# Attention stages of a two-layer trunk: accumulation banks by segment, a bank of their own for the value sums, and two places for other work per step

## The chip, the cores and the metric

The kernel runs on one core of one Trainium2 chip. The metric is the device time of one execution in microseconds (us); the time before is the median of three runs. TensorE is called PE, VectorE DVE, ScalarE ACT, GpSimd POOL, SyncE SP.

## What is computed

Two layers over 256 context tokens and 512 latent tokens, 1024 channels, all in 32-bit floats. Cut to what matters here:

```python
for l in range(2):
    h = rmsnorm(x) * (1 + scale) + shift               # latent and context tokens
    u, q, k, v, hq, hi, zf, zb, hgate, g_pool, g_attn, g_hg = split(h @ w_in[l])
    q, k = rope(rmsnorm(q)), rope(rmsnorm(k))            # 8 query heads of 64, 2 key heads
    a = softmax(q k^T / 8) v                             # latent queries: all 768 keys; context queries: 256
    y = (sigmoid(g_pool) * (pool_mix(u) @ w_bp) + sigmoid(g_attn) * (a @ w_ba)
         + sigmoid(g_hg) * (hgrn(hq, hi, zf, zb, hgate) @ w_bh)) @ w_out[l]
    x = x + gate * y
    x = x + gate2 * swiglu(rmsnorm(x) * (1 + scale2) + shift2)
```

In layer 0 both token groups are carried on (T = 768 columns); of layer 1 only the latent tokens are wanted (512 columns).

## The kernel before

Activations are kept transposed, 128 channels by tokens, so a product is a sum over eight tiles of 128 channels. Each 32-bit factor is split into a rounded part `hi` and a rest `lo` (ACT casts, DVE subtracts, `load_w` and `split`), and a product takes three matmuls (`mm3`, L261): hi x hi, lo x hi, hi x lo. One output tile of 128 channels over 512 columns is therefore 24 matmuls, and `gemm_h` gives control back after each three.

PE's order is written out by hand: PE executes in the order of the program. The other engines are ordered by a scheduler. To keep PE busy while DVE and ACT work, the program keeps a queue of other products: the branch products of the recurrent mixer (`merge` with `w_bh`, tiles `boh`) and the gate products of the attention branch (`early_gates`), whose tanh is stored to DRAM (`tdr`) and read back in the last merge. `fill(us)` issues as many from the queue as the cost says; the amounts are in the table `PACE`.

There are eight PSUM banks of 512 columns. The pool `pa` (tag "att") has four; the pool `pg` (tag "g") holds two double banks for a product over both segments in layer 0 (`wide`), and four single banks in layer 1.

Attention goes over four pairs of heads p. For a pair, `attn_pv` walks over jobs, one for each block of 128 keys and, in layer 0, one for the context queries: `score` (four matmuls, L673 and L674, then the exponential on ACT, L675), `hooks`, then `value` (the sums with v, L683, into one bank of `pa` that is held for the whole pair). Within `hooks(i)`, once per step, stands what belongs to the next pair: the split of its queries (`attn_max` to its first yield, L607 on ACT), its score maxima over the context keys (L620, four matmuls of 256 columns into two banks, then two reduces L622 on DVE) and over the latent keys (L628, two of 512 columns, reduces L630), two such pieces in each of steps 0 to 3 and the rest in step 4; then the maxima's rows (L646), the next projection of queries, and the filler.

After the last pair, `attn_out` sums the exponentials (L763, copied on ACT L764), divides and splits (L273 and L274) into `boa`. Then the last `merge` (`w_ba`) goes over eight output tiles: tanh of the gate (from DRAM, or from a gate product made there where none was ready), 12 branch matmuls, a product with the gate on DVE (L825), an addition on POOL (L827) to the sum so far that is read back from DRAM (`ybuf`), and a split into `y`. The output projection (`grouped`, L1064) needs all eight y for each of its tiles.

## Time and profile before

| | |
|---|---|
| median of 3 runs | 2167.5 us (2167.08 to 2168.65) |
| the profiled execution's own time | 2168.29 us |
| its span | 2166.5 us |
| PE busy | 2087.3 us (96%) |
| DVE, ACT, POOL busy | 51%, 32%, 7% |
| layer 0's attention steps | some 398 to 579 us |
| layer 1's attention steps | some 1559 to 1712 us |
| layer 1's last merge, then the output projection | from 1720 us, from 1753.4 us |

A row of a timeline is one instruction: when it starts, how long its record lasts, and in brackets how long its engine stood idle before it and what ended that. Records of matmuls overlap: what a matmul costs in a stream is the distance between starts. A row of waits is a sum over a stretch.

### The profile page before, as it was taken

What the parts mean: (1) busy time and instruction counts of PE and PEld (TensorE: products, weight loads), DVE (VectorE), ACT (ScalarE), POOL (GpSimd) and SP (SyncE); (2) the same over time, 40 slices, a digit from 0 to 9 for tenths busy, and PEclk for the clock granted to TensorE, in tenths of its full rate; (3) what the DMA queues carried; (4) which work ended last, traced back from release to release, by engine and by line L of the source; (5) the groups of instructions that cost most, each with busy time, mean ns of one, the idle gap of its engine ahead of it and who ended that gap; (6) DMA issues with size and microseconds to landing.
All of it is one profiled execution on the core that took longest, in us unless ns stands there. A gap on an engine that the chain in (4) does not pass through costs nothing.

```text
span 2166.5 us, 28558 instructions
## 1 busy us (share of the span) xinstructions
PE 2087.3 (96%) x11844; PEld 1696.6 (78%) x11844; DVE 1102.7 (51%) x1615; ACT 691.2 (32%) x968; POOL 147.4 (7%) x153
## 2 busy tenths in 40 slices
...
GB/s 280 89 30 103 187 164 90 50 69 59 109 121 143 88 138 161 101 88 156 139 66 106 91 81 74 57 65 97 88 73 63 111 188 86 96 98 93 99 93 97
DMA packets 74018, 226.74 MB, mean 105 GB/s; under 512 B 8272, under 2 KB 8416, under 8 KB 73760
## 3 DMA queue, kind: packets, MB, share of 16 engines
...
## 4 chain that ended last, share of the span: by engine, by line
PE 85%; DVE 7%; ACT 3%; DMA 2%; issue 2%; POOL 1%; SPq 0%; POOLq 0%; DVEq 0%; ACTq 0%
PE g L261 63%; PE g L1064 5%; PE att L683 3%; PE att L367 2%; PE g L1020 2%; PE att L1064 2%; DMA ada<-in_w_ada_dram 2%; PE att L673 1%; PE att L424 1%; DVE AT L463 1%; PE att L674 1%; PE att L173 1%; PE att L628 1%; DVE lo L243 1%; PE att L1020 1%
## 5 line engine op out<-in xcount | busy, mean ns | idle before, releaser
L261 PE MATMUL g<-h,hi 128*128 128x512 f32 (+1 forms) x3840 | 991.9, 361 | 9.1 <-ACT h L319 2.6
L261 PEld LDWEIGHTS g<-h,hi 128*128 128x128 f32 x3840 | 680.1, 189 | 146.9 <-issue 26.0
L261 PE MATMUL g<-h,lo 128*128 128x512 f32 (+1 forms) x1920 | 571.1, 355 | 0.2 <-DVE lo L243 0.2
L241 ACT CAST hi<-raw 128x1024 fp32r<-128x1024 f32 (+1 forms) x237 | 245.3, 1036 | 830.1 <-PE g L261 526.1
L243 DVE TENSOR_TENSOR lo<-raw,hi 128x1024 fp32r<-128x1024 f32 (+1 forms) x237 | 285.4, 1206 | 330.2 <-ACT hi L241 327.6
L261 PEld LDWEIGHTS g<-h,lo 128*128 128x128 f32 x1920 | 363.3, 189 | 53.2 <-issue 1.7
L261 PE MATMUL g<-uh,hi 128*128 128x512 f32 (+1 forms) x416 | 130.4, 360 | 0.0
L261 PE MATMUL g<-ul,hi 128*128 128x512 f32 (+1 forms) x416 | 130.4, 360 | 0.0
L261 PE MATMUL g<-uh,lo 128*128 128x512 f32 (+1 forms) x416 | 130.3, 360 | 0.0
L1078 DVE SCALAR_TENSOR_TENSOR x<-g,mod,x 128x256 f32<-128x256 f32 (+1 forms) x64 | 42.4, 682 | 166.5 <-PE g L261 146.8
L980 DVE TENSOR_TENSOR sa<-sa,g 128x512 f32<-128x512 f32 (+1 forms) x43 | 35.1, 818 | 171.1 <-PE g L261 169.9
L675 ACT ACTIVATE e<-att 128x512 f32<-128x512 f32 x104 | 56.6, 595 | 124.5 <-PE att L674 124.5
L214 DVE SCALAR_TENSOR_TENSOR junk<-adar,cb 128x1024 f32<-128x1024 f32 x64 | 78.2, 1222 | 34.1 <-DMA adar<-in_w_adaT_dram 33.2
L261 PEld LDWEIGHTS g<-ul,hi 128*128 128x128 f32 x416 | 78.2, 188 | 12.5
L261 PEld LDWEIGHTS g<-uh,lo 128*128 128x128 f32 x416 | 78.2, 188 | 12.4
L261 PEld LDWEIGHTS g<-uh,hi 128*128 128x128 f32 x416 | 78.2, 188 | 12.4
L827 POOL TENSOR_TENSOR ybuf<-ybuf,tanh 128x768 f32<-128x768 f32 (+1 forms) x32 | 57.8, 1807 | 388.9 <-DVE tanh L825 261.2
L324 POOL TENSOR_TENSOR h<-nsq,h 128x256 fp32r<-128x256 f32 (+1 forms) x32 | 34.3, 1075 | 734.5 <-ACT nsq L323 734.4
L683 PE MATMUL att<-e,Vv 128*64 128x512 f32 (+1 forms) x224 | 56.8, 592 | 0.0
L463 DVE COPY_PREDICATED AT<-masks,att 128x512 f32<-128x512 uint8 (+1 forms) x84 | 48.8, 630 | 13.2 <-PE att L424 13.0
L424 PE MATMUL att<-qq,K 64*128 64x128 f32 x560 | 42.8, 292 | 8.5 <-DVE qq L452 6.1
L677 DVE TENSOR_TENSOR tot<-tot,e 128x1024 f32<-128x1024 f32 x32 | 39.1, 1221 | 22.1 <-ACT e L675 21.9
...
## 6 DMA issues: line engine op xcount, KB each, us to landing
...
ada<-in_w_ada_dram SPq DMA_DIRECT2D x64, 256.0 KB, 3.6
...
ada<-in_w_ada_dram SPq DMA_DIRECT2D x16, 512.0 KB, 10.1
...
```

The costliest lines, as they stand in the source:

```text
L214: i = nc.vector.scalar_tensor_tensor(out=junk, in0=raw, scalar=1.0, in1=cb[:, v, :], op0=ALU.mult, op1=ALU.mult, accum_out=rows[:, f, v:v ...
L241: nc.scalar.copy(hi, raw)
L243: nc.vector.tensor_sub(lo, raw, hi.bitcast(F32))
L261: nc.tensor.matmul(ps.part(s0, s1), w, x[:, s0:s1], start=(first and i == 0), stop=(last and i == 2))
L367: nc.tensor.matmul(ps[:, :384], self.h[x][kk][:, c], w[:, kk, :], start=(kk == 0 and i == 0), stop=(kk == KD - 1 and i == 2))
L424: nc.tensor.matmul(pt[hd][:, i, :], K(ph, g0 + i), Q(ph, g0 + i), start=True, stop=True)
L463: scores(plain(K), lambda ph, c: pick(qq, c * P, P, h, ph), grow, lambda o, i, n: nc.vector.copy_predicated(o, mk.to_broadcast([P, n, P]), i))
L675: nc.scalar.activation(e[:, o, :], pst, AF.Exp, scale=0.125)
L683: nc.tensor.matmul(out[64 * o:64 * o + 64, :n], w(sk), es[i][:, o, u * n:(u + 1) * n], start=(start and u == 0), stop=(stop and u == len(j ...
L827: nc.gpsimd.tensor_add(y[:, c0:], y[:, c0:], th[:, c0:])
L1020: nc.tensor.matmul(o, w[:, kk, :], self.h[x][kk][:, tg[0]:tg[1]], start=(kk == 0 and i == 0), stop=(kk == KD - 1 and i == 2))
L1064: self.nc.tensor.matmul(ps, w[:, i, :], xs[y][:, g0:g1], start=(i == 0 and k == 0), stop=(i == nk - 1 and k == 2))
```

## The change

The banks. A method `banks(wide)` opens either two double banks, or three single ones and one bank for the value sums (pool `pv`). The narrow form holds in layer 0's attention and in all of layer 1; so `pa` has all four banks for scores, maxima and the sums of exponentials.

The products. `product` replaces the loops of `gemm_h` and `branch`. With narrow banks and a function `take` (what evacuates the result) it makes one segment, evacuates it, and then makes the next; so in layer 0's attention the products over 768 columns run as 24 matmuls of 256 columns and then 24 of 512, instead of alternating. In layer 1 a product without `take` still opens both of its segments at once.

The places. `hooks(i, half)` is called before and after `value`; each half fills half the amount. The split of the queries stands in (0, 0), the first piece of the maxima in (1, 0), one piece in each half up to (4, 0), the rest in (4, 1), the rows in (5, 0) and the projection in (5, 1).

The amounts: 'att' from (1.7, 1.5) to (2.4, 2.2), 'head' from (2.0, 0.6) to (1.5, 1.0), 'last' from (1.5, 1.2) to (1.0, 0.8), for layers 0 and 1. The norms of k and of the first q take their scratch from the buffers "e" in place of "ntmp".

```diff
-PACE = {'hn': 3.5, 'gap': (6.4, 10.2), 'hg': (2.9, 2.6), 'att': (1.7, 1.5), 'head': (2.0, 0.6), 'last': (1.5, 1.2), 'tail': (7.0, 5.0)}
+PACE = {'hn': 3.5, 'gap': (6.4, 10.2), 'hg': (2.9, 2.6), 'att': (2.4, 2.2), 'head': (1.5, 1.0), 'last': (1.0, 0.8), 'tail': (7.0, 5.0)}
...
-        self.pg = self.pgs.enter_context(tc.tile_pool(name="pg", bufs=2, space=bass.MemoryType.PSUM))
-        self.wide = True
+        self.banks(True)
...
+    def banks(self, wide):
+
+        self.pgs.close()
+        self.pg = self.pgs.enter_context(self.tc.tile_pool(name=self.nm("pg"), bufs=2 if wide else 3, space=bass.MemoryType.PSUM))
+        if not wide:
+            self.pv = self.pgs.enter_context(self.tc.tile_pool(name=self.nm("pv"), bufs=1, space=bass.MemoryType.PSUM))
+        self.wide = wide
...
-    def gemm_h(self, w, segs):
-
-        hi, lo = w
-        ps = self.acc(segs)
-        for kk in range(KD):
-            self.mm3(ps, hi[:, kk, :], lo[:, kk, :], self.h[0][kk], self.h[1][kk], segs, kk == 0, kk == KD - 1)
-            yield 3 * sum(s1 - s0 for s0, s1 in segs) / 2370.0
+    def product(self, w, xs, nk, segs, take=None):
+
+        ps = None
+        for part in (segs,) if self.wide or take is None else [(x,) for x in segs]:
+            ps = self.acc(part)
+            for kk in range(nk):
+                self.mm3(ps, w[0][kk], w[1][kk], xs[0][kk], xs[1][kk], part, kk == 0, kk == nk - 1)
+                yield 3 * sum(s1 - s0 for s0, s1 in part) / 2370.0
+            for x in ps if take is not None else ():
+                take(*x)
         return ps
+
+    def gemm_h(self, w, segs, take=None):
+        return self.product([[x[:, kk, :] for kk in range(KD)] for x in w], self.h, KD, segs, take)
...
-    def headnorm(self, dst, src, c0, w, pool, tag, tagr):
-
-        nc = self.nc
-        sq = self.t(pool, [P, T], F32, tag, bufs=2 if tag == tagr else None)
+    def headnorm(self, dst, src, c0, w, scratch):
+
+        nc = self.nc
+        sq = scratch(0)
         nc.scalar.activation(sq[:, c0:], src[:, c0:], AF.Square)
         self.fill(PACE['hn'])
-        r = self.t(pool, [P, T], F32, tagr, bufs=2 if tag == tagr else None)
+        r = scratch(1)
...
-                pvs[s0] = self.t(self.pa, [P, 512], F32, "att")
+                pvs[s0] = self.t(self.pv, [P, 512], F32, "pv")
...
         score(0)
-        hooks(0)
+        hooks(0, 0)
+        hooks(0, 1)
         score(1)
         for i in range(len(jobs)):
-            hooks(i + 1)
+            hooks(i + 1, 0)
             value(i)
+            hooks(i + 1, 1)
             if i + 2 < len(jobs):
                 score(i + 2)
...
-            def hooks(i):
-                if i > 0:
+            def hooks(i, half):
+                if i > 0 and half == 0:
                     next(late, None)
-                if i == 5:
+                if (i, half) == (5, 0):
                     self.now(late)
                 if nxt is not None:
-                    if i < 4:
+                    if (i, half) < (4, 1) and i + half != 1 or (i, half) == (1, 0):
                         next(nxt, None)
-                        next(nxt, None)
-                    elif i == 4:
+                    elif (i, half) == (4, 1):
                         for _ in nxt:
                             pass
-                    elif i == 5:
+                    elif (i, half) == (5, 0):
                         state["s"] = self.attn_rows(p + 1, full)
-                if i == 5 and p < 2:
+                if (i, half) == (5, 1) and p < 2:
                     state["q"] = self.now(qproj(p + 2))
-                if i == 3 and p == 0:
+                if (i, half) == (3, 1) and p == 0:
                     self.attn_kv(1, k, ap)
-                self.fill(F if nxt is not None else FL)
+                self.fill(0.5 * (F if nxt is not None else FL))
...
-        ps = yield from self.gemm_h(w, self.segs(full))
-        t = self.t(pool, [P, T], F32, "tanh", bufs=2)
-        for s0, s1, a in ps:
-            self.nc.scalar.activation(t[:, s0:s1], a, AF.Tanh, scale=0.5)
-        return t
-
-    def branch(self, w, col, nk, bo, full):
-        ps = self.acc(self.segs(full))
-        hi, lo = w
-        for kk in range(nk):
-            self.mm3(ps, hi[:, kk, col:col + P], lo[:, kk, col:col + P], bo[0][kk], bo[1][kk], self.segs(full), kk == 0, kk == nk - 1)
-            yield 3 * sum(s1 - s0 for s0, s1 in self.segs(full)) / 2370.0
-        return ps
+        t = Lazy(lambda: self.t(pool, [P, T], F32, "tanh", bufs=2))
+
+        def take(s0, s1, a):
+            self.nc.scalar.activation(t.get()[:, s0:s1], a, AF.Tanh, scale=0.5)
+        yield from self.gemm_h(w, self.segs(full), take)
+        return t.get()
+
+    def branch(self, w, col, nk, bo, full, take):
+        return self.product([[x[:, kk, col:col + P] for kk in range(nk)] for x in w], bo, nk, self.segs(full), take)
...
-                ps = yield from self.with_ada(self.branch(wb, (e % per) * P, nk, bo, full))
                 t = y if prev is None else th
-                for s0, s1, a in ps:
+
+                def take(s0, s1, a):
                     nc.vector.scalar_tensor_tensor(out=t[:, s0:s1], in0=th[:, s0:s1], scalar=1.0, in1=a, op0=ALU.add, op1=ALU.mult)
+                yield from self.with_ada(self.branch(wb, (e % per) * P, nk, bo, full, take))
...
+        self.banks(False)
...
-        ps = self.now(self.gemm_h(self.load_w(W[21], [P, KD, P]), self.segs(True)))
-        for s0, s1, a in ps:
-            nc.scalar.copy(k[:, s0:s1], a)
-        self.headnorm(k, k, 0, self.v(l, O_KN, 1), at, "ntmp", "ntmp")
-        self.rope_lat(k, at, "ntmp")
+        self.now(self.gemm_h(self.load_w(W[21], [P, KD, P]), self.segs(True), lambda s0, s1, a: nc.scalar.copy(k[:, s0:s1], a)))
+
+        def early(i):
+            return self.t(at, [P, 2, 512], F32, "e", bufs=3).rearrange("p a b -> p (a b)")[:, 0:T]
+
+        def later(i):
+            return self.t(at, [P, T], F32, "ntmp", bufs=2)
+        self.headnorm(k, k, 0, self.v(l, O_KN, 1), early)
+        self.rope_lat(k, later)
 
         def qproj(i):
+            scratch = early if i == 0 else later
             q = self.t(at, [P, T], F32, "q")
-            ps = yield from self.gemm_h(self.load_w(W[22 + i], [P, KD, P]), segs)
-            for s0, s1, a in ps:
-                nc.scalar.copy(q[:, s0:s1], a)
-            self.headnorm(q, q, c0, self.v(l, O_QN, 1), at, "ntmp", "ntmp")
-            self.rope_lat(q, at, "ntmp")
+            yield from self.gemm_h(self.load_w(W[22 + i], [P, KD, P]), segs, lambda s0, s1, a: nc.scalar.copy(q[:, s0:s1], a))
+            self.headnorm(q, q, c0, self.v(l, O_QN, 1), scratch)
+            self.rope_lat(q, scratch)
...
         self.attention(l, k, qproj, full, at, bo_a)
         self.fill(PACE['tail'][l])
         ready.stop = True
         self.finish()
+        if full:
+            self.banks(True)
...
 
         accs = []
         for i in range(len(ws)):
-            if i < 2 or not self.wide:
+            if i < (2 if self.wide else 3):
                 accs.append(self.acc(segs))
             else:
                 accs.append(Acc([(s0, s1, self.t(self.pa, [P, 512], F32, "att")[:, 0:s1 - s0]) for s0, s1 in segs]))
...
         def second(wsrc):
-            self.pgs.close()
-            self.pg = self.pgs.enter_context(tc.tile_pool(name="pg1", bufs=4, space=bass.MemoryType.PSUM))
-            self.wide = False
+            self.banks(False)
             ps = [self.acc(self.segs(False)) for _ in wsrc]
             self.gemm_part([self.load_w(w, [P, KD, P]) for w in wsrc], [p.part(LC, T) for p in ps], (LC, T))
```

How PE's order changes in layer 1's attention steps (pair p, second place with maxima over the context keys). `qs` are the split queries of the next pair, `khh` the keys, `g` a filler bank, `h` and `boh` factors of fillers, `e` and `Vv` those of the value sums. Before:

```order
8040 L620 MATMUL att_12611<-khh_1858_12283,qs_1913_12546 128x256
8041 L620 MATMUL att_12612<-khh_1858_12283,qs_1914_12547 128x256
8042 L628 MATMUL att_12619<-khh_1858_12283,qs_1913_12546 128x512
8043 L628 MATMUL att_12620<-khh_1858_12283,qs_1914_12547 128x512
8044 L261 MATMUL g_12526<-h_1471_10142,hi_12522 128x512
8045 L261 MATMUL g_12526<-h_1471_10142,lo_12524 128x512
8046 L261 MATMUL g_12526<-h_1479_10150,hi_12522 128x512
8047 L261 MATMUL g_12632<-boh_1538_10525,hi_12307 128x512
```

After:

```order
8024 L633 MATMUL att_12653<-khh_1893_12361,qs_1948_12624 128x256
8025 L633 MATMUL att_12654<-khh_1893_12361,qs_1949_12625 128x256
8026 L268 MATMUL g_12604<-h_1501_10208,hi_12600 128x512
8027 L268 MATMUL g_12604<-h_1501_10208,lo_12602 128x512
8028 L268 MATMUL g_12604<-h_1509_10216,hi_12600 128x512
8029 L268 MATMUL g_12604<-h_1502_10209,hi_12600 128x512
8030 L268 MATMUL g_12604<-h_1502_10209,lo_12602 128x512
8031 L268 MATMUL g_12604<-h_1510_10217,hi_12600 128x512
8032 L696 MATMUL pv_12667<-e_12615,Vv_10594 64x512 x2
8033 L641 MATMUL att_12670<-khh_1893_12361,qs_1948_12624 128x512
8034 L641 MATMUL att_12671<-khh_1893_12361,qs_1949_12625 128x512
```

The maxima over latent keys (512 columns) followed those over context keys (256 columns) directly; now six filler products and a value sum stand between, and the value sum goes to its own bank.

How DVE's order changes in layer 1's last merge. `tanh` rows are the products with the gate, `y` rows the last step of a tile, `lo` rows splits of weights. Before:

```order
1191 L825 SCALAR_TENSOR_TENSOR tanh_13572<-tanh_13572,g_13584 128x512
1192 L274 TENSOR_TENSOR y_2138_13561<-ybuf_13582,y_2130_13553 128x512
1193 L825 SCALAR_TENSOR_TENSOR tanh_13574<-tanh_13574,g_13605 128x512
1194 L243 TENSOR_TENSOR lo_13701<-raw_13697,hi_13699 128x1024
1195 L274 TENSOR_TENSOR y_2139_13562<-ybuf_13603,y_2131_13554 128x512
1196 L825 SCALAR_TENSOR_TENSOR tanh_13601<-tanh_13601,g_13632 128x512
1197 L274 TENSOR_TENSOR y_2140_13563<-ybuf_13630,y_2132_13555 128x512
1198 L825 SCALAR_TENSOR_TENSOR tanh_13622<-tanh_13622,g_13653 128x512
1199 L243 TENSOR_TENSOR lo_13753<-raw_13749,hi_13751 128x1024
1200 L274 TENSOR_TENSOR y_2141_13564<-ybuf_13651,y_2133_13556 128x512
```

After:

```order
1207 L835 SCALAR_TENSOR_TENSOR tanh_13718<-tanh_13718,g_13730 128x512
1208 L242 TENSOR_TENSOR lo_13870<-raw_13866,hi_13868 128x1024
1209 L835 SCALAR_TENSOR_TENSOR tanh_13720<-tanh_13720,g_13751 128x512
1210 L287 TENSOR_TENSOR y_2183_13707<-ybuf_13728,y_2175_13699 128x512
1211 L287 TENSOR_TENSOR y_2184_13708<-ybuf_13749,y_2176_13700 128x512
1212 L835 SCALAR_TENSOR_TENSOR tanh_13747<-tanh_13747,g_13778 128x512
1213 L242 TENSOR_TENSOR lo_13942<-raw_13938,hi_13940 128x1024
1214 L835 SCALAR_TENSOR_TENSOR tanh_13768<-tanh_13768,g_13799 128x512
1215 L287 TENSOR_TENSOR y_2185_13709<-ybuf_13776,y_2177_13701 128x512
1216 L287 TENSOR_TENSOR y_2186_13710<-ybuf_13797,y_2178_13702 128x512
1217 L242 TENSOR_TENSOR lo_13974<-raw_13970,hi_13972 128x1024
```

A product and the y of the tile before it took turns; now two products come, then two y. On PE, the eight branch products of this merge stood in three groups (60, 12 and 24 matmuls) with a gate product of 24 between each; now all 96 stand in a row, and before them 24 instead of 36 filler matmuls follow the last sum of exponentials.

How PE's order changes in layer 1's recurrent mixer, where one projection (`g` numbers 1588 and 1589, then 1621 and 1622) is followed by the next. A `waits` in brackets is a semaphore that the instruction waits for. Before:

```order
L261 MATMUL g_1588_10793<-h17_1479_10150,hi_1586_10789 128x256
L261 MATMUL g_1589_10794<-h17_1479_10150,hi_1586_10789 128x512
L261 MATMUL g_1593_10851<-h00_1464_10135,hi_1591_10847 128x256
L261 MATMUL g_1594_10852<-h00_1464_10135,hi_1591_10847 128x512
L261 MATMUL g_1593_10851<-h00_1464_10135,lo_1592_10849 128x256
L261 MATMUL g_1594_10852<-h00_1464_10135,lo_1592_10849 128x512
```

After:

```order
L268 MATMUL g_1621_10863<-h17_1510_10217,hi_1619_10859 128x256
L268 MATMUL g_1622_10864<-h17_1510_10217,hi_1619_10859 128x512
L268 MATMUL g_1626_10921<-h00_1495_10202,hi_1624_10917 128x256
L268 MATMUL g_1627_10922<-h00_1495_10202,hi_1624_10917 128x512 [waits Activation_49]
L268 MATMUL g_1626_10921<-h00_1495_10202,lo_1625_10919 128x256
L268 MATMUL g_1627_10922<-h00_1495_10202,lo_1625_10919 128x512
```

The second projection's first 512-column matmul now waits for ACT, which it did not before.

## Rows read from the trace of the kernel before

**Rows 1.** The page: busy us (share) x instructions, PE and weight loads.

```profile
PE 2087.3 (96%) x11844; PEld 1696.6 (78%) x11844; DVE 1102.7 (51%) x1615; ACT 691.2 (32%) x968; POOL 147.4 (7%) x153
```

**Rows 2.** Stretches: from:to, us, busy by engine, granted clock, DMA share.

```profile
440.00:480.00 40.00, 38.25 (x188) 23.69 (x187) 31.75 (x45) 17.69 (x28) 4.52 (x3) 1.00 0.22 75
...
1604.00:1624.00 20.00, 18.29 (x59) 9.87 (x59) 14.07 (x19) 6.27 (x12) 1.26 (x1) 0.83 0.11 39
1652.00:1664.00 12.00, 10.12 (x30) 5.94 (x32) 7.29 (x10) 5.69 (x9) 0.36 (x1) 0.72 0.25 85
```

**Rows 3.** Tile of maxima, layer 0: count, min/median/max ns, first and last start.

```profile
L630 DVE TENSOR_REDUCE mx<-att x24: 678/680/692, 406.9 to 529.6; 128x1 f32<-128x512 f32 x24
```

**Rows 4.** PE's waits, 320 to 600 us: line, releaser, total, times, longest.

```profile
PE att L620 <- DVE mx L630: 3.4, 3, 1.5
PE att L628 <- DVE mx L622: 2.8, 2, 2.1
```

**Rows 5.** The same view, 1490 to 1740 us (layer 1's attention).

```profile
PE att L620 <- ACT qs L607: 5.2, 3, 3.1
...
PE att L628 <- DVE mx L622: 4.1, 5, 1.4
```

**Rows 6.** PE's timeline, two places of maxima: start, us, operation, idle before.

```profile
464.45 0.38 PE L620 MATMUL att<-khh,qs 64*128 64x256 f32 x1
466.31 0.50 PE L620 MATMUL att<-khh,qs 64*128 64x256 f32 x3 [1.48 <-DVE mx L630]
466.74 0.61 PE L261 MATMUL g<-h,hi 128*128 128x256 f32 x2
...
1547.77 0.50 PE L620 MATMUL att<-khh,qs 64*128 64x256 f32 x4
1548.20 0.50 PE L261 MATMUL g<-h,hi 128*128 128x512 f32 x1
1548.54 0.39 PE L261 MATMUL g<-h,lo 128*128 128x512 f32 x1
```

**Rows 7.** PE's timeline: ends of an alternating stretch, then of a 256-column stretch.

```profile
646.29 0.51 PE L261 MATMUL g<-h,hi 128*128 128x256 f32 x2
...
654.61 0.51 PE L261 MATMUL g<-boa,hi 128*128 128x256 f32 x2
...
708.03 0.28 PE L1064 MATMUL att<-y,hi 128*128 128x256 f32 x1
...
713.70 0.59 PE L307 MATMUL att<-nacc,cm 128*128 128x512 f32 x1
```

**Rows 8.** ACT's timeline, layer 1's recurrent mixer: first projection's short segment.

```profile
1342.76 0.39 ACT L382 ACTIVATE k<-g 128x256 f32<-128x256 f32 x1
```

**Rows 9.** Layer 1's merge: timelines by engine, one DMA row (landing us).

```profile
1711.84 0.59 ACT L764 COPY sm<-att 128x512 f32<-128x512 f32 x1 [0.25 <-PE att L763]
...
1718.39 0.69 DVE L274 TENSOR_TENSOR boa<-ntmp,boa 128x512 fp32r<-128x512 f32 x1 [0.69 <-ACT boa L273]
...
1720.03 0.40 PE L261 MATMUL g<-boa,hi 128*128 128x512 f32 x1
...
1725.11 1.29 POOL L827 TENSOR_TENSOR ybuf<-ybuf,tanh 128x512 f32<-128x512 f32 x1 [72.75 <-DMA ybuf<-ydr]
1728.50 2.21 POOL L827 TENSOR_TENSOR ybuf<-ybuf,tanh 128x512 f32<-128x512 f32 x1 [2.10 <-DVE tanh L825]
...
1740.47 1.29 POOL L827 TENSOR_TENSOR ybuf<-ybuf,tanh 128x512 f32<-128x512 f32 x1 [2.11 <-DVE tanh L825]
...
1754.98 1.28 POOL L827 TENSOR_TENSOR ybuf<-ybuf,tanh 128x512 f32<-128x512 f32 x1 [2.11 <-DVE tanh L825]
...
1756.95 0.69 DVE L274 TENSOR_TENSOR y<-ybuf,y 128x512 fp32r<-128x512 f32 x1 [2.10 <-ACT y L273]
...
1756.97 0.39 PE L1064 MATMUL g<-y,hi 128*128 128x256 f32 x1 [0.92 <-ACT y L273]
...
ybuf<-ydr SPq DMA_DIRECT2D x8, 256.0 KB, 3.3
```

6 lines of the change are left out of this document (3 added, 3 removed).

## The prediction

> **What bounds the kernel now.** I read the busy times of the page first: TensorE (PE) is busy 2087.3 us [rows 1] of a span of 2166.5 us, in a profiled run of 2168.29 us. So only about 79 us of idle PE can be won at all, and PE's matmuls are as many after the change as before. What the change can move is the idle time in the two attention stages, the clock there, and what the new order does to the stages behind them. The list of PE's waits comes next. In layer 0's attention (320 to 600 us) the two largest entries are matmuls of the score maxima that wait for a reduce on VectorE (DVE): 3.4 and 2.8 us [rows 4]. In layer 1's (1490 to 1740 us) it is 4.1 us of the same kind and 5.2 us in which the first maxima of a head pair wait for ScalarE's (ACT) copy of the queries [rows 5]. The timeline of one place shows the mechanism: a group of four 256-column products has one product through, then PE stands 1.48 us until the reduce of the previous pair gives its bank back [rows 6]. A reduce takes 0.68 us [rows 3], and the values' sum holds one of the four banks, so only three serve scores and maxima. Last I asked for the granted clock by stretch: two stretches of layer 1's steps fall to means of 0.83 and 0.72 of full speed [rows 2]; both contain such waits.
>
> **What the change removes.**
>
> Maxima. The named waits are 3.4 + 2.8 + 4.1 = 10.3 us [rows 4, 5]. Each costs more than its name: from the start of the broken group at 464.45 to the first filler product at 466.74 are 2.29 us, where the same four products take 0.43 us elsewhere (1547.77 to 1548.20) [rows 6]; so 1.86 us are lost for 1.48 named, a factor of 1.26. That makes 13.0 us. After the change a group follows filler, not another group, and has one bank more; but each half place now carries only half the filler, and DVE has the same reduces to do. I take a quarter as left: **-9.8 us**. Bounds: 0 (DVE is what binds, see the rivals) and -13.0.
>
> Queries. Before, the split of a pair's queries and its first maxima are issued in the same place, with nothing between, so PE waits for the copy: 5.2 us in three waits [rows 5]. After, the copy is issued at (0, 0) and the first maxima at (1, 0): two half fillers and a score group lie between, over 2 us of PE work. I leave half a microsecond: **-4.7 us**, bounds -3 and -5.2.
>
> Clock. The two stretches lose 20 x 0.17 + 12 x 0.28 = 6.8 us of full-clock time; PE was busy 18.29 + 10.12 of their 32 us, so 6.0 us of it fell on work [rows 2]. Both lie in stretches with waits that go. I take **-5 us**, bounds 0 and -6.
>
> Sum of the gains: -19.5 us.
>
> **What it adds.**
>
> Segments. In layer 0's attention some 490 pairs of matmuls that ran as 256 and 512 columns in alternation run one segment after the other. In alternation a pair costs (654.61 - 646.29) / 24 = 0.347 us; a stream of 256-column products costs (713.70 - 708.03) / 48 = 0.118 us [rows 7]. A separate 512-column product cannot cost more than two of these, so a separated pair costs at most 0.354: 0 to 7 ns more, 0 to 3.5 us. Layer 1 streams at 512 columns without trouble, so I take **+1 us**.
>
> Switches. The first product after a group of another kind holds PE 0.34 us (1548.20 to 1548.54) against 0.23 for one in a stream (0.347 less 0.118) [rows 6, 7]: 0.11 us each. By the order, some 15 such switches more: **+1.6 us**, bounds 0 and 2.
>
> Banks in layer 1. Three single banks stand where four stood, also outside the attention. The recurrent mixer's two projections take two banks each: the second one's 512-column start now waits for the first one's 256-column bank, which a 0.39 us activation empties [rows 8]; the order shows the new wait. With the way there and back I take 0.75 us for each of two places: **+1.5 us**, bounds 0.4 and 3. In the output projection and the feed-forward a group of 24 products takes 5.5 us and its bank needs one short DVE step, so two banks in hand still cover it: nothing; if that cover were gone, it would be under a microsecond for each of some forty groups, which I don't expect.
>
> Layer 0's lead-in and merge. The fillers there are given by cost, so their number changes a little, and five gates are ready rather than four. DVE is busy 31.75 of 40 us in that stage [rows 2], so a little is lost when a chain isn't covered: **+1 us**, bounds 0 and 2.
>
> Layer 1's tail: the largest cost. The larger fillers finish all eight early gates within the steps. Before, two gates (48 products, some 11 us) were left and stood between the eight branch products; now 96 branch products stand in a row. The gate work is not lost, it moved ahead; but it covered a chain. Time from the copy of the sums at 1711.84. The last split ends at 1718.39 + 0.69, 7.2 us on [rows 9]. 24 filler products (5.5 us) remain in front, so PE stands about 1.7 us. Then the branches: 96 x 0.23 = 22.1 us, to 29.3, and the first 21 products of the output projection at 0.118, to 31.8: there PE needs the last of the eight y. The chain that makes it: the first GpSimd (POOL) add starts 5.1 us after the first branch (1720.03 to 1725.11), so at 12.3. Then seven more, at a pace: before it was (1740.47 - 1725.11) / 4 = 3.84 us each, with filler enough between. At best it is set by the two ybuf buffers: a load lands 3.3 us after issue, and from an add's start to the end of the y are 1756.95 + 0.69 - 1754.98 = 2.66 us, so 5.96 us for two, 2.98 each [rows 9]. DVE's new order goes by pairs (two products, then two y, with weight splits between), neither the one nor the other; I take 3.5. The last y is ready at 12.3 + 7 x 3.5 + 2.7 = 39.5 (35.9 at 2.98, 41.9 at 3.84). PE stands 7.7 us (4.1 to 10.1); with the 1.7 in front, less the 0.92 that it stood there before [rows 9], that is +8.5 (4.9 to 10.9). A stand of that length can bring the clock down as in layer 1's steps, at most by the 3.4 us of one such stretch [rows 2]; I take 1. **+9.5 us**, bounds 4.9 and 14.3.
>
> On the same adds: one took 1.29 us and the next 2.21 us, while DVE ran a subtraction, a product and a weight split beside it [rows 9]. The Trainium skill, page "SBUF — State Buffer", section "SBUF: two separate sides", says that VectorE with two SBUF inputs and GpSimd take a shared port pair as an exclusive lock, and the loser blocks; the 2.21 us agree with that. By it, work that DVE does in denser bunches would lengthen more of the eight adds, by up to 0.9 us each, 4 us over the tail if half are hit.
>
> **Sum.** -19.5 + 1 + 1.6 + 1.5 + 1 + 9.5 = -4.9 us. Against the profiled run's 2168.3 us that is 2163.4; that run lies 0.8 us above the median 2167.5 of the timed runs, so **2162.6 us**. A measurement of this kernel can tell about 0.2% from no change, 4.3 us either way of 2167.5: 2163.2 to 2171.8.
>
> **Rivals.**
>
> The tail is hidden: loads come early enough and the chain keeps within the 2.8 us of a branch, so y7 is there when PE comes. For it: the reloads can be issued during the steps. Against: the two buffers alone make 2.98. All 9.5 us go: 2153. Chance 0.15.
>
> No difference: the gains are as summed, but the tail stands at its upper end, pace 3.84 and the clock falls (+14.3 in place of 9.5). For it: 3.84 was measured, and with gates between, so with less pressure. That gives 2167.4. Chance 0.20.
>
> Slower, by one mechanism: DVE, not the banks, sets when the maxima can go. DVE is at 31.75 of 40 us in layer 0's steps [rows 2], and 24 reduces of 0.68 us [rows 3] are 16.3 us of that stage, and 18 more, over the context keys, come on top. If the reduces come late because DVE has other work queued, a fourth bank and another place only move the wait; the 9.8 us don't come, nor the 5 us of clock that hang on them. Then -4.7 + 14.6 = +9.9: 2177. It decides against the change as soon as less than half of the maxima's 9.8 and none of the clock comes. Against it: 8 of the 40 us are free, and the wait in the timeline ends with one reduce, not several. Chance 0.17.
>
> Slower, by weight loads. They take 1696.6 us for 11844 [rows 1], 143 ns in the mean, more than the 118 ns of a 256-column product; if a load could not be hidden behind so short a product, 490 pairs would lose 25 ns each, 12 us, in place of the 1 us taken: 2174. The stream of 48 at 0.118 [rows 7] loads new weights for each product and shows none of it. Chance 0.02. The Trainium skill, page "TensorE: Matmul & The Clock Gate", section "Back-to-back issue gap", says that the spacing of such a stream is set by both load and product; the 0.118 us say that here the product sets it.
>
> That the change doesn't do what it says I leave out: the order shows values in their own bank, halves and segments.
>
> **Chances.** Forecast 0.46, hidden tail 0.15, no difference 0.20, DVE 0.17, weight loads 0.02. The forecast lies just past the border of what can be told, so it gives about 0.27 to faster and 0.17 to same, 0.02 to slower; the hidden tail gives 0.15 to faster; no difference gives 0.17 to same, 0.03 to faster; the slower ones 0.17 and 0.02. Faster 0.45, same 0.34, slower 0.21. The range: from 2153 (hidden tail; beyond it lie a tenth) to 2174 (the DVE case's better half; beyond it a tenth): 2153 to 2174.
>
> **What would show it.** Waits of maxima for a reduce: 3 to 4 us together in both layers, from 10.3; the wait for the queries' copy gone; a granted clock near 1.00 in layer 1's steps; PE's span of the two attention stages shorter by the sum of these. In layer 1's tail one long wait of PE for the last y, 4 to 10 us, and a short one for the last split. Two new waits of about 0.75 us in layer 1's recurrent projections. I am wrong if the maxima's waits stay with DVE busy throughout, if the tail's wait is missing or over 10 us, or if a separated pair in layer 0's attention costs more than 0.354 us.

## The result and the profile after

The changed kernel takes 2179.5 us (median of four runs, 2175.86 to 2181.64), against 2167.45 of the kernel before: a ratio of 1.0051 (95% interval 1.0039 to 1.0064). The forecast was 2162.6 with a range of 2153 to 2174: the time moved the other way and lies outside the range. The profiled run took 2181.64 us, 13.35 more than the profiled run before. The runs further down were timed in three other sets, each together with the kernel before, whose median there was 2168.6 to 2169.3; their ratios are to that median, so compare ratios rather than times. One execution of all, of the run with the larger amounts alone, took 2925 us at a granted clock of 0.65 and is left out of its ratio.

PE's busy time is only 3.2 us longer, so most of the difference is idle time; the clock is in the busy time too. The head of the page after, the span and the line that answers to [rows 1]:

```profile
span 2179.9 us, 28621 instructions
...
PE 2090.5 (96%) x11844; PEld 1700.1 (78%) x11844; DVE 1110.6 (51%) x1623; ACT 695.0 (32%) x986; POOL 145.2 (7%) x153
```

To find where it went, I cut both timelines of PE at the same instructions and, for each stage, took from its length what its matmuls would take back to back (counts by the order, pitches as in [rows 7] and 0.230 us for 512 columns). What is left I call the loss of a stage: idle time, low clock and switches. It can be compared although the change moves filler between stages. The absolute loss holds some coarse pitches; its difference between kernels is what counts. A lead-in runs from the end of the mixer before it. Loss in us, worked out from the timelines:

| stage | before | after | difference | forecast |
|---|---|---|---|---|
| layer 0, lead-in to the first scores | 31.4 | 39.0 | +7.6 | +1 with the merge |
| layer 0, steps (first scores to last sums) | 46.5 | 38.8 | -7.7 | |
| layer 0, last merge | 0.2 | 3.4 | +3.2 | |
| layer 1, mixer (from the feed-forward before it) | | | +2.2 | +1.5 |
| layer 1, lead-in to the first scores | 24.4 | 30.1 | +5.7 | 0 |
| layer 1, steps | 48.3 | 43.6 | -4.7 | |
| layer 1, last merge and output projection | | | +7.7 | +9.5 |
| both layers' steps together | | | -12.4 | -19.5, with +2.6 for segments and switches |

With -0.7 before the first attention that makes +13.3, the whole of it. The sums come out the same without any pitches where stages are taken together, for then the kernels have the same matmuls: from the first scores of layer 0 to its output projection are 263.6 us before and 259.0 after (-4.6, the table has -4.5), from the first scores of layer 1 to the end of its output projection 239.0 and 242.0 (+3.0, as in the table).

The two lead-ins are the surprise. Waits of PE in the changed kernel, first from 320 to 606 us, then from 1470 to 1570 us (waiting line, releaser, total, times, longest). In the kernel before, neither the waits for `ybuf` nor the 1.6 us for `tanh` stand there; the last line does, as L337 with 4.3 us:

```profile
PE g L268 <- DVE ybuf L835: 4.1, 1, 4.1
PE g L268 <- ACT tanh L793: 1.6, 1, 1.6
```

```profile
PE g L268 <- DVE ybuf L835: 4.2, 1, 4.2
PE att L350 <- ACT ntmp L344: 4.0, 1, 4.0
```

And the place in layer 0, in order of time on DVE and PE:

```profile
330.46 0.95 DVE L835 SCALAR_TENSOR_TENSOR ybuf<-tanh,g 128x768 f32<-128x768 f32 x1 [0.72 <-DMA ydr<-ybuf]
...
331.46 0.39 PE L268 MATMUL g<-h,hi 128*128 128x256 f32 x1 [4.07 <-DVE ybuf L835]
```

The matmul at 331.46 is the first of the projection of k, the first product after `banks(False)`. It waits until DVE has emptied the last bank of the old pool, and DVE waits in turn for the store of the one `ybuf`. DVE is no later than it was: this write ends 4.4 and 4.5 us (layers 0 and 1) after the start of the last matmul ahead of the switch, and in the kernel before 4.5 and 4.2 us, where PE went on to the projection of k meanwhile. Then the clock falls. The stretch of the lead-in before and after (granted clock third from the end of the row), then the four microseconds behind each of the two waits after:

```profile
320.00:400.00 80.00, 75.68 (x398) 61.31 (x398) 51.08 (x73) 33.66 (x40) 12.53 (x15) 0.98 0.22 72
```

```profile
320.00:400.00 80.00, 72.55 (x359) 58.68 (x358) 45.21 (x65) 33.69 (x44) 12.77 (x14) 0.90 0.21 71
```

```profile
332.00:336.00 4.00, 4.00 (x23) 4.00 (x22) 0.00 (x0) 0.00 (x0) 1.34 (x4) 0.57 0.48 186
1503.00:1507.00 4.00, 3.55 (x18) 3.58 (x19) 2.36 (x4) 0.62 (x1) 0.72 (x2) 0.57 0.49 185
```

The mean falls by 0.08 over 80 us, the idle time among them. The lead-in of layer 0 loses 7.6 us more, of which 4.1 are this wait, that of layer 1 5.7 with a wait of 4.2. The stretches at 0.57 lose 1.7 us of full-clock time each. With them the wait accounts for 5.8 us in layer 0 and for all of it in layer 1; the rest in layer 0 lies between the first maxima and the first scores, where the clock is at its lower level, 0.50, for 13.6 us and was for 3.4 before. The 1.6 us for `tanh` is the switch back, at layer 0's last merge.

In layer 1's steps the old waits went, but others came. [rows 5] had 5.2 us for the queries' copy and 4.1 for reduces (2.9 of it in the steps proper); after, from 1572 to 1730 us:

```profile
PE att L633 <- ACT e L688: 4.1, 2, 2.1
PE att L659 <- DVE m L650: 2.9, 1, 2.9
PE att L633 <- ACT qs L620: 0.6, 1, 0.6
```

The first maxima of a pair now meet banks held by exponentials (`e`), and the transposition of the maxima (L659) comes right behind the last reduce. The clock fell again, to 0.91 and 0.83, as it had before [rows 2]; over the whole of the steps it reads 0.95 before (first row) and 0.96 after (second):

```profile
1561.70:1711.20 149.50, 141.20 (x536) 82.46 (x535) 95.11 (x129) 60.80 (x96) 10.68 (x10) 0.95 0.21 69
...
1571.90:1730.50 158.60, 150.74 (x597) 90.93 (x595) 100.09 (x132) 65.42 (x101) 12.18 (x10) 0.96 0.23 75
1610.00:1630.00 20.00, 17.22 (x66) 9.91 (x64) 12.85 (x17) 10.87 (x16) 3.09 (x2) 0.91 0.20 65
...
1650.00:1670.00 20.00, 19.33 (x69) 12.95 (x70) 5.92 (x9) 6.21 (x7) 0.12 (x1) 0.83 0.25 76
```

Layer 1's tail cost about what was forecast, though by other parts (see below). POOL's first six adds come in pairs at a pace of 7.0 us, PE waits for a product of the merge and then for y, and the clock falls to 0.83 (POOL, PE, then the stretch):

```profile
1744.98 2.54 POOL L838 TENSOR_TENSOR ybuf<-ybuf,tanh 128x512 f32<-128x512 f32 x2 [70.40 <-DMA ybuf<-ydr]
1752.11 2.54 POOL L838 TENSOR_TENSOR ybuf<-ybuf,tanh 128x512 f32<-128x512 f32 x2 [4.59 <-DVE tanh L835]
1758.90 2.51 POOL L838 TENSOR_TENSOR ybuf<-ybuf,tanh 128x512 f32<-128x512 f32 x2 [4.25 <-DMA ybuf<-ydr]
...
1766.71 1.26 POOL L838 TENSOR_TENSOR ybuf<-ybuf,tanh 128x512 f32<-128x512 f32 x1 [0.43 <-DMA ybuf<-ydr]
```

```profile
1758.16 0.49 PE L268 MATMUL g<-boa,hi 128*128 128x512 f32 x1 [1.85 <-DVE tanh L835]
1766.98 0.39 PE L1081 MATMUL g<-y,hi 128*128 128x256 f32 x1 [2.06 <-ACT y L286]
1768.58 0.50 PE L1081 MATMUL g<-y,hi 128*128 128x256 f32 x2 [1.09 <-DVE y L287]
```

```profile
1755.00:1775.00 20.00, 14.79 (x75) 12.66 (x74) 12.15 (x15) 6.35 (x10) 5.04 (x4) 0.83 0.79 261
```

### The profile page after: what moved, and what is told of

It reads as the page before. It is cut to its first block, busy times and chain, and to the rows that moved or that the text cites. A ratio compares the mean times of both kernels' runs of the same rounds, so it can differ in the third digit from the quotient of the medians.

```text
span 2179.9 us, 28621 instructions
## 1 busy us (share of the span) xinstructions
PE 2090.5 (96%) x11844; PEld 1700.1 (78%) x11844; DVE 1110.6 (51%) x1623; ACT 695.0 (32%) x986; POOL 145.2 (7%) x153
## 4 chain that ended last, share of the span: by engine, by line
PE 62%; DVE 5%; ACT 2%; issue 1%; DMA 1%; POOL 1%; SPq 0%; DVEq 0%; POOLq 0%
PE g L268 48%; PE g L1081 5%; PE g L1037 2%; PE att L1081 2%; PE att L380 1%; PE pv L696 1%; PE att L1037 1%; DVE lo L242 1%; DMA ybuf<-ydr 1%; PE att L437 1%; ACT hi L240 1%; DVE nsq L331 0%; PE att L686 0%; PE att L687 0%; DVE st L508 0%
## 5 line engine op out<-in xcount | busy, mean ns | idle before, releaser
L268 PE MATMUL g<-h,hi 128*128 128x512 f32 (+1 forms) x3840 | 1022.2, 363 | 18.5 <-DVE ybuf L835 8.3
L268 PE MATMUL g<-h,lo 128*128 128x512 f32 (+1 forms) x1920 | 598.9, 356 | 0.0
L997 DVE TENSOR_TENSOR sa<-sa,g 128x768 f32<-128x768 f32 (+1 forms) x42 | 34.5, 822 | 170.7 <-PE g L268 169.5
L688 ACT ACTIVATE e<-att 128x512 f32<-128x512 f32 x104 | 56.4, 595 | 107.8 <-PE att L687 105.2
L268 PEld LDWEIGHTS g<-uh,hi 128*128 128x128 f32 x416 | 78.2, 188 | 12.4
L268 PEld LDWEIGHTS g<-uh,lo 128*128 128x128 f32 x416 | 78.2, 188 | 12.4
L337 POOL TENSOR_TENSOR h<-nsq,h 128x256 fp32r<-128x256 f32 (+1 forms) x32 | 34.2, 1072 | 735.7 <-ACT nsq L336 735.6
L696 PE MATMUL pv<-e,Vv 128*64 128x512 f32 (+1 forms) x224 | 58.8, 610 | 0.5 <-ACT ntmp L707 0.5
L476 DVE COPY_PREDICATED AT<-masks,att 128x512 f32<-128x512 uint8 (+1 forms) x84 | 48.9, 632 | 13.4 <-PE att L437 13.3
L268 PE MATMUL g<-boa,hi 128*128 128x256 f32 (+1 forms) x192 | 50.0, 365 | 3.5 <-DVE tanh L835 1.8
```

The costliest lines, as they stand in the source:

```text
L268: nc.tensor.matmul(ps.part(s0, s1), w, x[:, s0:s1], start=(first and i == 0), stop=(last and i == 2))
L476: scores(plain(K), lambda ph, c: pick(qq, c * P, P, h, ph), grow, lambda o, i, n: nc.vector.copy_predicated(o, mk.to_broadcast([P, n, P]), i))
L688: nc.scalar.activation(e[:, o, :], pst, AF.Exp, scale=0.125)
L696: nc.tensor.matmul(out[64 * o:64 * o + 64, :n], w(sk), es[i][:, o, u * n:(u + 1) * n], start=(start and u == 0), stop=(stop and u == len(j ...
```

## The experiments

The theory after the result: the switch of the pools costs the two lead-ins (A), the row of branch products costs the tail (C), and in the steps something other than the bank binds. Losses below are in us, by the same cut.

**No second opening in layer 1.** The narrow form holds already when layer 1's attention begins; the change closes and opens it all the same.

```diff
-        self.banks(False)
+        if self.wide:
+            self.banks(False)
         self.attn_setup(at)
```

> The narrow banks are not closed and opened again at layer 1's attention (they are narrow already); layer 0 still switches. Theory A, the switch itself: PE's wait of 4.2 us for DVE's write of ybuf at the start of layer 1's attention goes, and with it the low clock behind it; the lead-in of layer 1 is 5.6 us shorter than in the changed kernel, total about 2174 us; the wait of 4.1 us in layer 0 stays. Theory B, DVE is late there anyway (ybuf has one buffer and DVE waits for its store): the wait of 4.2 us stays whatever the pools do, total 2179.5 us.

Measured: 2176.32 us (ratio 1.0038, 1.0023 to 1.0053). Layer 1's lead-in (the mixer's last score products to the first maxima) took 75.7 us, as before (75.8), against 81.4. Layer 0's kept its wait. In this run the first waits from 1465 to 1566 us are:

```profile
PE att L350 <- ACT ntmp L344: 4.1, 1, 4.1
PE att L641 <- DVE mx L635: 1.9, 2, 1.1
```

Theory A stands: DVE's write ends 4.7 us after the start of the matmul ahead of it, no sooner than in the changed kernel, and PE doesn't wait for it; it is the opening that makes PE wait. Of the 5.7 us in this stretch, the median shows 3; the runs differ by a few us in the mixer (1.3 us longer here in the profiled run), which the lead-in's own length doesn't hold.

**The projection of k in two pa banks.** The pools are switched, but nobody needs the new ones at once.

```diff
-        self.now(self.gemm_h(self.load_w(W[21], [P, KD, P]), self.segs(True), lambda s0, s1, a: nc.scalar.copy(k[:, s0:s1], a)))
+        hi, lo = self.load_w(W[21], [P, KD, P])
+        for s0, s1 in self.segs(True):
+            ka = Acc([(s0, s1, self.t(self.pa, [P, 512], F32, "att")[:, 0:s1 - s0])])
+            for kk in range(KD):
+                self.mm3(ka, hi[:, kk, :], lo[:, kk, :], self.h[0][kk], self.h[1][kk], ((s0, s1),), kk == 0, kk == KD - 1)
+            nc.scalar.copy(k[:, s0:s1], ka.part(s0, s1))
```

> The pools are switched as in the changed kernel, but the projection of k, which comes first after the switch, accumulates in two of the four pa banks, which are idle there; the filler after it then is the first to use the new banks, 8.4 us later. Theory A (the switch): both waits go, the lead-ins get 5.6 and 5.8 us shorter, about 2168 us. Theory B (DVE late anyway, bound by its chain): DVE's last product ends as late as before, but nobody needs it within 8.4 us, so the waits go too, about 2168 us; only if DVE is later than that a wait stands at the first filler.

Measured: 2166.89 us (0.9989, 0.9975 to 1.0002). Both lead-ins to the first maxima are back, 138.7 (before 138.6, after 144.7) and 75.7. The two lead-ins are 11.7 us shorter together, and the medians differ by 12.6 (by the ratios some 13): about the whole loss against the kernel before. DVE's writes end as late as before, so this run alone could not tell the switch from a late DVE; the run before it can.

**The old amounts of filler.**

```diff
-PACE = {'hn': 3.5, 'gap': (6.4, 10.2), 'hg': (2.9, 2.6), 'att': (2.4, 2.2), 'head': (1.5, 1.0), 'last': (1.0, 0.8), 'tail': (7.0, 5.0)}
+PACE = {'hn': 3.5, 'gap': (6.4, 10.2), 'hg': (2.9, 2.6), 'att': (1.7, 1.5), 'head': (2.0, 0.6), 'last': (1.5, 1.2), 'tail': (7.0, 5.0)}
```

> Only the amounts of filler are those of the kernel before; banks, segments and places are of the changed kernel. Two gates are left for layer 1's last merge again. Theory C (the row of 96 branch products exposes the chain of the merge): the 3.4 us more from the first branch product to the output projection and the 3.9 us more within it go, 7.3 us. Against it stand the steps, which lose filler: if the gain of 12.3 us in the steps came from the filler, the steps lose most of it again and the total rises to about 2184 us; if it came from banks and places, the total is about 2173 us. I expect 2175.

Measured: 2188.52 us (1.0094, 1.0077 to 1.0110), worse than either of my numbers. The tail is back to what it was (33.3 and 47.5 us for merge and output projection, as before to 0.02), so C holds. But the steps lose 50.5 and 48.2, with banks and places of the changed kernel, where the kernel before lost 46.5 and 48.3 with the same amounts. The maxima's waits are gone there and the rows' wait has taken their place; waits in layer 0's steps, then the first of layer 1's:

```profile
PE att L659 <- DVE m L650: 8.1, 3, 3.9
PE att L633 <- ACT e L688: 0.5, 1, 0.5
```

```profile
PE att L659 <- DVE m L650: 5.2, 2, 2.8
```

So banks and places alone gain nothing; the wait moves to the next thing that needs the reduces. In layer 0 they even lose: from the first scores to the output projection, the switch back included, 270.9 us stand against 263.6 of the kernel before, with the same matmuls.

**One place per step, the rest as changed.** The calls `hooks(i, 0)` and `hooks(i, 1)` are one `hooks(i)` again, with the body of the kernel before.

```diff
-        hooks(0, 0)
-        hooks(0, 1)
+        hooks(0)
         score(1)
         for i in range(len(jobs)):
-            hooks(i + 1, 0)
+            hooks(i + 1)
             value(i)
-            hooks(i + 1, 1)
...
-                self.fill(0.5 * (F if nxt is not None else FL))
+                self.fill(F if nxt is not None else FL)
```

> The place for other work is one per step again, with the whole amount, as in the kernel before; banks, segments and amounts are of the changed kernel. If the fourth bank made the gain in the steps (12.3 us over both layers), it stays within 3 us: about 2180. If the two places made it, maxima over context and latent keys meet again and the waits for reduces come back, some 8 us: about 2187. In both cases layer 1's wait for the queries' copy comes back in part, since split and first maxima stand together again: 2 to 5 us of this.

Measured: 2184.66 us (1.0078, 1.0063 to 1.0093). The steps lose 41.6 in layer 0 (38.8 after) and 43.1 in layer 1 (43.6). The second place is worth 2.8 us in layer 0 and nothing in layer 1; the rest of the 5 us is not in the steps, and the runs of the changed kernel alone spread by 5.8. In layer 1 one wait took the place of another: the 4.1 us for exponentials are gone, and the wait for the queries' copy is back, as expected:

```profile
PE att L633 <- ACT qs L620: 3.4, 4, 1.6
```

**The kernel before with the larger amounts alone.** In the kernel before:

```diff
-PACE = {'hn': 3.5, 'gap': (6.4, 10.2), 'hg': (2.9, 2.6), 'att': (1.7, 1.5), 'head': (2.0, 0.6), 'last': (1.5, 1.2), 'tail': (7.0, 5.0)}
+PACE = {'hn': 3.5, 'gap': (6.4, 10.2), 'hg': (2.9, 2.6), 'att': (2.4, 2.2), 'head': (1.5, 1.0), 'last': (1.0, 0.8), 'tail': (7.0, 5.0)}
```

> The kernel before with nothing changed but the amounts of filler: those of the changed kernel. Theory D (the steps are bound by the chain of DVE and ACT, and filler only fills it): the steps lose as little as in the changed kernel, 39 and 44 us over bare PE time, from 46.5 and 48.3; 12 us gained, and 7.3 us of it given back in layer 1's tail, where eight branch products stand in a row here too: some 5 us faster than the kernel before, about 2162.5 us. Theory E (the larger amounts need the fourth bank and the two places): the steps gain less than half, 6 us or fewer, and with the tail the total is no faster than before, 2167 to 2170 us.

Measured: 2179.26 us (median of five; 1.0046, 1.0033 to 1.0059), slower than either theory's total. Theory E for layer 0, where the loss rises from 46.5 to 52.6; two reduces are waited for and the clock falls (PE, then two stretches):

```profile
472.98 0.79 PE L620 MATMUL att<-khh,qs 64*128 64x256 f32 x3 [2.13 <-DVE mx L630]
```

```profile
440.00:480.00 40.00, 37.84 (x182) 25.34 (x181) 29.93 (x36) 17.45 (x25) 5.86 (x3) 0.91 0.28 92
...
520.00:560.00 40.00, 38.07 (x169) 24.78 (x170) 28.83 (x38) 11.77 (x20) 3.68 (x2) 0.91 0.23 79
```

Theory D for layer 1: 44.4 against 48.3 before and 43.6 after. There filler alone made the gain, and the bank nearly none. The tail costs 9 us here too (56.4 us for the output projection in place of 47.5), without the new banks: it is the row of branches. Six us more in layer 0's steps, four less in layer 1's and nine more in the tail make about the 10 us by which the total is longer.

**The kernel before with the larger amounts and the two places.** Its own banks: the value sums in one of four, double banks in layer 0. On top of the run above:

```diff
-        hooks(0)
+        hooks(0, 0)
+        hooks(0, 1)
         score(1)
         for i in range(len(jobs)):
-            hooks(i + 1)
+            hooks(i + 1, 0)
             value(i)
+            hooks(i + 1, 1)
...
-                self.fill(F if nxt is not None else FL)
+                self.fill(0.5 * (F if nxt is not None else FL))
```

> The kernel before with the larger amounts of filler and with the two places per step, but with its own banks (the value sums hold one of four, double banks in layer 0). It completes a square for layer 0's steps at the larger amounts, in us over bare PE time: one place and old banks 52.6, one place and new banks 41.6, two places and new banks 38.8. If the banks (with the products by segment) make the gain and the places add 3 us, this reads 49 to 50, and the total is about 2176. If the places alone do it, it reads 39 to 42, total about 2167.

Measured: 2166.09 us (0.9990, 0.9981 to 1.0000). The loss of layer 0's steps is 41.7: not the 49 to 50 of the first reading, but the 39 to 42 of the second, and the total fits it too. The square at the larger amounts:

| layer 0's steps, loss | old banks | new banks and segments |
|---|---|---|
| one place | 52.6 | 41.6 |
| two places | 41.7 | 38.8 |

Either of the two takes away 11 us, and the second then adds 3. They don't add up, because they take away the same thing. In the upper left corner PE waits 4.0 us for reduces (3.6 and 0.4), and the two stretches at 0.91 lose 7.2 us of full-clock time: the 11 us. With either of the two the waits for reduces are 0.7 us or none, and no stretch of the steps is below 1.00 (here the wait, then the first of the two stretches, of this run):

```profile
PE att L628 <- DVE mx L630: 0.7, 1, 0.7
```

```profile
440.00:480.00 40.00, 38.76 (x200) 26.34 (x200) 32.61 (x40) 19.69 (x29) 6.40 (x3) 1.00 0.29 92
```

The 3 us that the new banks add in the steps are lost again in the last merge, where the old banks need no switch back: from the first scores to the output projection, with the same matmuls, this run takes 258.9 us and the changed kernel 259.0 (269.8 with one place and old banks, 261.8 with one place and new banks). So what the change wanted could be had without new banks, and without the switch that they bring. In layer 1 the steps lose some 42 here, and the wait for exponentials stands here too, with the old banks; it came with the places:

```profile
PE att L620 <- ACT e L675: 4.1, 2, 2.1
```

**Three mends together.** No second opening, k in pa, and the mixer's first projections segment by segment:

```diff
-            ps = yield from self.gemm_h(self.load_w(ws[dirn], [P, KD, P]), self.segs(True))
-            for s0, s1, a in ps:
+            def take(s0, s1, a):
                 nc.scalar.activation(k[:, dirn, s0:s1], a, AF.Sigmoid, scale=-1.0)
+            yield from self.gemm_h(self.load_w(ws[dirn], [P, KD, P]), self.segs(True), take)
```

> The changed kernel with three mends: narrow banks not opened again in layer 1, the projection of k in two pa banks, and the first projections of the recurrent mixer of layer 1 segment by segment, each emptied before the next (so that a bank comes free early). Theory A and the bank theory for the mixer: the two lead-ins 11.4 us shorter than in the changed kernel, the mixer of layer 1 2.2 us shorter: about 2165 us. If the mixer's 2.2 us are not from the banks, it stays as in the run with k in pa, 2167 us.

Measured: 2162.40 us (0.9974, 0.9964 to 0.9983). The changed kernel's wait in the mixer,

```profile
PE g L268 <- ACT k L395: 1.5, 1, 1.5
```

is gone. From layer 0's feed-forward to the mixer's last score products it took 730.6 us, against 734.3 after and 732.0 before. One run is little to go by, for that stretch read 728.8 in the run of the larger amounts, whose code there is the one of before. But all six profiled runs with this mend read 728.9 to 730.6, and the five with the changed kernel's code 731.0 to 735.8. These are mostly runs of other sets, so how much the mend is worth beyond the 1.5 us of the wait is open.

**A third buffer in the tail.** `tanh` and `ybuf` with three buffers in the last merge, on top of the three mends (`self.nb` is 2 elsewhere).

```diff
-                nth = self.t(pool, [P, T], F32, "tanh", bufs=2)
+                nth = self.t(pool, [P, T], F32, "tanh", bufs=self.nb)
...
-                y = self.t(pool, [P, T], F32, "ybuf", bufs=1 if ready is None else 2)
+                y = self.t(pool, [P, T], F32, "ybuf", bufs=1 if ready is None else self.nb)
...
         adp = ExitStack()
+        self.nb = 3
```

> The same with three buffers each for the tanh and the partial sum read back in the last merge, in place of two. Theory F (the chain in the tail is set by the reloads into two buffers): the pace falls from 7.0 us for two tiles to under 6.5, the 7.3 us that the tail costs shrink by 3 to 5: about 2161 us. If DVE's and POOL's order sets the pace, nothing: 2165 us.

Measured: 2158.63 us (0.9959, 0.9944 to 0.9973). Last merge and output projection of layer 1: 76.1 us against 77.5 in the run before it. It is 1.3 us, not 3 to 5, though the pace did change: from the first add on POOL to the last start 18.6 us in place of 21.2, and PE's named waits in the tail fell from 6.4 to 4.0 us. So the two buffers set part of the pace; the tail's code was the same in seven runs with two buffers, and they read 77.5 to 79.3. The totals differ by 3.8 us, but their intervals overlap.

**The maxima and their transposition half a step later**, on top of the three mends.

```diff
-                    if (i, half) < (4, 1) and i + half != 1 or (i, half) == (1, 0):
+                    if (i, half) < (4, 1) and i + half != 1 and (i, half) != (1, 0):
...
-                    elif (i, half) == (5, 0):
+                    elif (i, half) == (5, 1):
                         state["s"] = self.attn_rows(p + 1, full)
```

> The combination (without the third buffers) with the maxima's first piece half a step later and the transposition of the maxima half a step later. In the changed kernel's layer 1 the first maxima waited 4.1 us for exponentials that hold the banks and the rows 2.9 us for DVE. If these waits are from the places, they go: 5 to 7 us and some clock, about 2158 us; if DVE and ACT are late whatever the place, the waits move: 2165 us.

Measured: 2152.19 us (0.9923, 0.9911 to 0.9936), some 10 us less than with the three mends alone and 6 below what was expected. The loss of layer 1's steps falls from 40.9 to 33.6, which is 7.3 of it; the rest isn't located. The two waits are down to 1.3 and 0.4, and the clock stays up (waits, then the stretch of the steps):

```profile
PE att L659 <- DVE m L650: 1.3, 1, 1.3
...
PE att L633 <- ACT e L688: 0.4, 2, 0.2
```

```profile
1551.50:1699.60 148.10, 145.48 (x597) 88.59 (x595) 100.47 (x133) 65.24 (x101) 12.44 (x10) 1.00 0.26 83
```

That these waits were of the places is shown for the two moves together; they were not tried one by one.

**Layer 1's old amounts, on top of the later places.** Two gates are left for the last merge again.

```diff
-PACE = {'hn': 3.5, 'gap': (6.4, 10.2), 'hg': (2.9, 2.6), 'att': (2.4, 2.2), 'head': (1.5, 1.0), 'last': (1.0, 0.8), 'tail': (7.0, 5.0)}
+PACE = {'hn': 3.5, 'gap': (6.4, 10.2), 'hg': (2.9, 2.6), 'att': (2.4, 1.5), 'head': (1.5, 0.6), 'last': (1.0, 1.2), 'tail': (7.0, 5.0)}
```

> The combination with the later places, and in layer 1 the amounts of filler of the kernel before, so that two gates are left for its last merge. Theory C for the tail: the first branch product to the feed-forward takes 80.9 us for 144 products and the output projection, as in the kernel before, against 78.9 for 96: 9 us less stall. The steps of layer 1 have 60 products less; with the places moved they lost 33.6 us over bare PE time. If that stays, the total falls by 9 us to about 2143; if filler was what the steps needed, they lose 4 to 10 us more and the total is 2144 to 2153.

Measured: 2152.77 us (0.9927, 0.9912 to 0.9942), the same total. The tail is back to 33.3 and 47.5 us, some 9 less stall; the steps' loss rises from 33.6 to 39.5, 4.0 us of it waits for the transposition again. Theory C is right, and undoing it gains nothing that the total shows. By the stages there is a small gain: from layer 1's first scores to the end of its output projection, with the same matmuls, 230.2 us stand against 233.0; but these first scores, up to which the code is the same, come 3.7 us later in this profiled run.

**Three buffers and later places together.** Both edits above, on top of the three mends:

```diff
+        self.nb = 3
...
-                    elif (i, half) == (5, 0):
+                    elif (i, half) == (5, 1):
```

> The combination with the later places and with three buffers for tanh and partial sum in the last merge. The third buffers brought 1.3 us in the tail before; here the tail costs 9 us, so if the two buffers set its pace, 1 to 4 us: 2148 to 2151. If the order of DVE and POOL sets it, 2152.

Measured: 2150.32 us (0.9912, 0.9897 to 0.9927), the shortest median here, though its interval overlaps those of the other runs with the later places. The merge takes 22.4 us, about its bare time, and the output projection 52.0: 74.4 together, 4.5 less than the 78.9 of the run with the later places alone, and below all seven with two buffers. PE's waits in the tail are four, all for y, from 2.26 us down:

```profile
1738.13 0.39 PE L1090 MATMUL g<-y,hi 128*128 128x256 f32 x1 [2.26 <-ACT y L286]
1738.86 0.69 PE L1090 MATMUL g<-y,hi 128*128 128x256 f32 x2 [0.23 <-DVE y L287]
```

**The switch back after layer 0's last merge**, on top of the later places.

```diff
-        if full:
-            self.banks(True)
         atp.__exit__(None, None, None)
...
             pass
+        if full:
+            self.banks(True)
         adp.close()
```

> The combination with the later places; in layer 0 the double banks are opened again only after the last merge, not before it. The theory of the switch: PE's wait of 1.6 us for a tanh at the first branch product goes, with it some 2 us of the 3 us that the switch back costs; but the same wait for the last bank can come at the output projection, where the first product would wait for the last branch's product on DVE, 1 to 2 us. Total 2150 to 2153.

Measured: 2152.06 us (0.9924, 0.9910 to 0.9939). The wait of 1.6 us for the tanh is gone, and the stretch from the last sums to the first branch product took 14.3 us against 16.0; the merge behind it took 59.7 against 58.4. What was feared stands there, a wait before the first product of the output projection:

```profile
656.84 0.47 PE L1087 MATMUL g<-y,hi 128*128 128x512 f32 x1 [1.08 <-issue]
```

The two stretches together are 0.4 us shorter; no gain that the total shows.

## Why the prediction was wrong

**The step that failed** is a term put at next to nothing. "Layer 0's lead-in and merge" stands at +1 us for a changed number of fillers, and layer 1's lead-in has no term at all. The prediction costs the new banks by what waits on them in the steps and in the mixer; it never asks what it takes to close one pool and open another over the same banks. That cost 4.1 and 4.2 us of waiting and some clock behind each: 7.6 and 5.7 us up to the first scores, and layer 0's last merge, behind the switch back, lost another 3.2. Together 16.5 us, where the sum had +1. The run with k in pa and the one without the second opening show it for the lead-ins. For the 3.2 it is not shown: 1.6 is the wait at the switch back, but moving the switch won back only 0.4. The order could have told: the first matmul of the projection of k waits for DVE in the changed kernel. The prediction reads the order at the steps, the mixer and the tail only.

Between the forecast of -4.9 us and the +13.3 of the profiled runs lie 18.2. These stages are 15.5 of it, the steps, which gained less, 4.5, and the mixer 0.7; the tail, which cost 1.8 less, and the 0.7 before the first attention go the other way.

**Maxima.** -9.8 us was taken for a quarter left. The waits for reduces did go: 10.3 us in [rows 4, 5], 3.5 in all after. But the windows of those rows reach over the lead-ins, where the change moves no place: only 6.3 of the 10.3 us lie in the steps (3.4 and 2.9), and these went entirely; 4.0 lie in the lead-ins, and the 3.5 that are left are all there. Priced by its own rule from 6.3, the term is -6.0. And the rival "DVE sets it" was half true: what the reduces feed comes next, and the wait moved to the transposition, as the run with the old amounts shows most plainly (8.1 and 5.2 us). I had priced that rival as no gain at all; it was less gain. The steps gained 12.4 in all, where the sum of its terms was -16.9.

**Queries.** -4.7: the wait for the copy fell from 5.2 to 0.6, as said, but 4.1 us for exponentials' banks stood in the same place. The term was right and its place taken by a new wait that the prediction doesn't have: as I read the order, with the first maxima right after the second score group, two score banks and one bank of sums are in use. The wait is gone in the run with one place and stands with the old banks too, so it is of the places.

**Clock.** -5 us: nothing. Over layer 1's steps the clock reads 0.95 before and 0.96 after, some 7 us of full-clock time in either, and waits of 2 to 3 us remained. It came only with the later places, where no wait over 1.3 us is left (1.00).

**Segments, switches.** +2.6 is not separable as a sum: the steps of layer 0 with new banks and two places lose 2.9 us less than with old banks, so the two together cost no more than the bank brings. But the price of a separated pair can be read in the changed kernel. A stretch of 512 columns and the stretch of 256 behind it, 22 products from the first to the second row of each:

```profile
336.17 0.40 PE L268 MATMUL g<-h,lo 128*128 128x512 f32 x1
341.18 0.51 PE L268 MATMUL g<-h,hi 128*128 128x512 f32 x2
341.51 0.28 PE L268 MATMUL g<-h,lo 128*128 128x256 f32 x1
344.15 0.52 PE L268 MATMUL g<-h,hi 128*128 128x256 f32 x2
```

That is 0.228 and 0.120 us, 0.348 for a pair, where alternation took 0.347 [rows 7]: the segments cost next to nothing, and the rival of weight loads, 25 ns a pair, is refuted.

**Banks in the mixer.** +1.5, measured 1.5 in the wait and 2.2 in the stage.

**Layer 1's tail.** +9.5, measured 7.7 (bounds 4.9 and 14.3), in part by luck. The first add came 8.4 us after the first branch product (1736.55 to 1744.98), not 5.1, since the partial sum's load was issued only at 1739.97. The pace of 3.5 us for a tile held for the first six adds (7.0 for two), but the last two came closer, and the seven steps took 21.7 us, not 24.5; so the last add began 30.2 us after the first branch product, and 29.6 was forecast. PE's named waits are 5.2 us, of which 1.85 are in the merge itself, 4.1 more than before and not 8.5; and the low clock costs 3.4 us (20 us at 0.83), not 1. The stall in front, 1.7 us, didn't show. By the rule of the Trainium skill that the prediction quotes (page "SBUF — State Buffer", section "SBUF: two separate sides") a denser order could have lengthened the adds on POOL. It didn't: the pairs took 2.54 us, 1.27 for one, and none took the 2.21 of [rows 9]. The trace doesn't speak against the rule, for here DVE was the loser. The first y of each pair starts while an add runs and takes 1.1 us, the last 1.56, where a y alone takes 0.69; the row of the last pair, 2.39 us for two, begins 0.25 us after the add at 1766.71:

```profile
1766.96 2.39 DVE L287 TENSOR_TENSOR y<-ybuf,y 128x512 fp32r<-128x512 f32 x2 [1.89 <-ACT y L286]
```

What stays open: the 39 us of loss that remain in layer 0's steps are not explained. The named waits in it sum to 1.5 us after, PE is busy for 182.4 of 184 us (406 to 590), and the pitches by which it is worked out are coarse. Open, too, is what the rest of the 3.2 us of layer 0's last merge is.
